# Another order of stages for the experts of a mixture layer, on one core

## The chip, the cores and the metric

The kernel runs on one core of one Trainium2 chip. The metric is the device time of one execution, in microseconds (us). Before the change it is 1570.87 us, the median of 3 runs (1569.34 to 1571.96). All rows below come from one profiled execution, which took 1567.68 us; its span, from the first to the last instruction, is 1565.9 us.

## The reference

One encoder layer on 512 tokens of width 1024, in float32: two groups of attention heads, cross-attention into 256 memory tokens, and a mixture of 32 experts. Only the last part is touched. Each token goes to its 4 best experts:

```python
logits = x @ w_router + b_router
top_logits, top_idx = lax.top_k(logits, 4)
gates = softmax(top_logits)
# for each expert e, over the tokens that chose it:
gu = xb @ w_gate_up[e] + b_gate_up[e]          # 1024 -> 2048
gate, up = split(gu); gate = min(gate, 7); up = clip(up, -7, 7)
y = ((up + 1) * gate * sigmoid(1.702 * gate)) @ w_down[e] + b_down[e]   # 1024 -> 1024
out[token] += gate_of(token, e) * y
```

An expert has 12 MiB of weights, and each of the 32 is read whole from the device's main memory.

## The kernel before

The layer's front part ends near 478 us. From there the 32 experts follow one another, one expert a stage. Experts are ranked by how many tokens chose them. A string, `PLAN` (line 34), names the kind of each stage, and `_rank` (line 36) deals the ranks out: the biggest experts to the stages of kind D, then E, W, M, N and Q, within a kind in the order of their stages. A kind says how many slots for tokens the stage has (`KINDS`, line 33): D 256, E 128+32, W 128, M 64+32, N 64, Q 32. Stage 0 is a W for one fixed expert.

Narrow stages (M, N, Q; class `NarrowStage`) multiply in plain float32 straight from the weights as they land, with 64 or 32 slots side by side in the array. A wide stage (W, E, D; `WideStage`, `DoubleStage`) first splits every row of weights into a high and a low part, `eh` on ScalarE (ACT, line 342) and `el` on VectorE (DVE, line 343), and does three products for each (lines 1424 to 1426).

A stage's weights are 12 chunks of 1 MiB (`wchunk`): eight of `w_gu` (gate and up), four of `w_dn` (down). SyncE (SP) issues their loads in order (line 1355), into 12 buffers in rotation, so that a load waits until the chunk 12 places before it has been used: in a narrow stage by the last product that reads it, in a wide stage by the split. While stage s runs, the loads of stage s+1 are issued, and the first ones of s+2. Behind a W or E, the last two chunks of a narrow stage go into other buffers (`load_late`, line 1658).

On TensorE (PE) the order is written by hand (`run_stage`, line 1670). A stage is: eight or more pieces of the up product, the activation (`act`: lines 1397 to 1400 on ACT and DVE), the transposes of its result `h` (`turn`), and the down product. The tokens' rows for the next stage are transposed three pieces before the end of the up product (`prep`). To cover the activation, the next stage's first pieces are done ahead: some before `turn`, some before the down product. This needs room in the six accumulators of 2 KiB per partition (PSUM banks):

```python
AHEAD = {"Q": (3, 1), "N": (2, 1), "M": (2, 2), "W": (1, 1), "E": (1, 1), "D": (1, 0)}   # 42
BANKS = {"Q": 1, "N": 2, "M": 3, "W": 4, "E": 5, "D": 4}                                  # 44
    if s in (0, len(PLAN) - 1, len(PLAN)) or BANKS[PLAN[s - 1]] + BANKS[PLAN[s]] > 6:     # 53
        return 0, 0
```

So a W gets two pieces ahead behind an N or a Q, and none behind an M or a W. The other engines' orders are set by a scheduler. With the plan before, the stages without pieces ahead are 11 (W behind M), 21 (W behind M), 22 (W behind W) and the last. In every fourth stage (s % 4 == 1) the tables of slots for four later stages are made beside the up product.

Of the kernel before, what the change touches and what calls it, by code (L numbers as in the profile page):

```python
# [30 lines left out]


KINDS = {"D": (2, 0, 0), "E": (1, 0, 1), "W": (1, 0, 0), "M": (0, 1, 1), "N": (0, 1, 0), "Q": (0, 0, 1)}
PLAN = "WNQDQNQEQMMWQMNMQNMQMWWNWNWNNMQQ"
_left = list(range(31))
_rank = {k: iter([_left.pop(0) for _ in range(PLAN.count(k) - (k == "W"))]) for k in "DEWMNQ"}
STAGES = [(k, 31 if i == 0 else next(_rank[k])) for i, k in enumerate(PLAN)]

# [11 lines left out]
def ahead(s):  # L50


    if s in (0, len(PLAN) - 1, len(PLAN)) or BANKS[PLAN[s - 1]] + BANKS[PLAN[s]] > 6:
        return 0, 0
    return AHEAD[PLAN[s]]


def ahead_chunks(s):

    n = sum(ahead(s))  # L60
    return 1 + max(k for _, k in PIECES[2 if PLAN[s] == "M" else 1][:n]) if n else 0


CAP = {k: 128 * v[0] + 64 * v[1] + 32 * v[2] for k, v in KINDS.items()}
assert PLAN[-1] == "Q" and sorted(r for _, r in STAGES) == list(range(32))

# [1812 lines left out]
```

## Time and profile before

| | |
|---|---|
| median of 3 runs | 1570.87 us |
| profiled execution, its span | 1567.68 us, 1565.9 us |
| PE busy | 1414.9 us (90%) |
| DVE, ACT, POOL busy | 48%, 35%, 11% |
| moved by DMA | 474.76 MB, mean 303 GB/s |
| loads of `wchunk` | 256 + 128 of 1 MiB |

How to read it: busy time is counted for each engine, and "idle before" is the time in which an engine stood still before an instruction, with the one that released it. Matmuls are pipelined, so a busy PE may still be slowed. From the slice at 470 us on, the load of the weights runs beside the stages. A stage is taken here to end where ACT begins its last copy of the result, `ys<-gu` (lines 140, 294 and 1496); with that the stages from 7 on are:

| stage | kind | from, us | stage | kind | from, us |
|---|---|---|---|---|---|
| 7 | E | 718.3 | 20 | M | 1137.4 |
| 8 | Q | 772.9 | 21 | W | 1177.5 |
| 9 | M | 788.4 | 22 | W | 1222.8 |
| 10 | M | 825.2 | 23 | N | 1265.5 |
| 11 | W | 859.9 | 24 | W | 1298.0 |
| 12 | Q | 902.0 | 25 | N | 1334.4 |
| 13 | M | 918.3 | 26 | W | 1367.5 |
| 14 | N | 954.4 | 27, 28 | N, N | 1403.9 |
| 15 to 19 | M Q N M Q | 978.8 | 29 to 31 | M Q Q | 1453.3 |

### The profile page before, as it was taken

The numbers are of one execution on the slowest core, as the hardware profiler recorded it, in microseconds if no ns is written. First come the engines' busy times: TensorE is split into PE (matmuls) and PEld (weight loads), VectorE is DVE, ScalarE is ACT, GpSimd is POOL, SyncE is SP. The second block draws the span as 40 slices with busy tenths as digits, with TensorE's granted clock in tenths as the row PEclk, the third lists the DMA queues.
The fourth block names the chain that finished last, engine by engine and source line by source line (L and its number), as shares of the span: only waits on it lengthen the run. The fifth ranks groups of instructions, "written<-read, shape, count | busy, mean of one in ns | idle before, by whom it ended". The sixth has DMA issues, their size and how long they took to land. (4 is left out here: it accounts for less than half of the span.)

```text
span 1565.9 us, 24737 instructions
## 1 busy us (share of the span) xinstructions
PE 1414.9 (90%) x9775; PEld 934.7 (60%) x9775; DVE 754.8 (48%) x1207; ACT 554.9 (35%) x799; POOL 175.2 (11%) x153
## 2 busy tenths in 40 slices
PE   8999999899998989978999999878888989899962
PEld 6898899788996557625644743323336756463321
DVE  6667797865478536225422720110118846462005
ACT  6667584444225333214301611000115645351001
POOL 1000000310031010020011011111002000111014
PEclk9999999999999999999999999999989999999975
DMA  6121245242449998799999999999999899999994
GB/s 214 43 66 58 73 133 192 68 150 80 189 173 375 392 396 323 270 404 418 405 416 388 409 406 412 416 412 416 412 411 389 335 408 357 398 362 354 416 412 179
DMA packets 111766, 474.76 MB, mean 303 GB/s; under 512 B 12577, under 2 KB 47801, under 8 KB 64032
## 3 DMA queue, kind: packets, MB, share of 16 engines
q1 hardware_dynamic: 98464, 446.66, 71.8%
q0 software_dynamic: 10848, 21.99, 5.3%
q10 hardware_dynamic: 2336, 4.50, 0.8%
q8 instruction: 78, 1.28, 0.3%
q14 instruction: 40, 0.33, 0.1%
HBM read 460.87 MB, written 17.32 MB: 305 GB/s over the span
## 5 line engine op out<-in xcount | busy, mean ns | idle before, releaser
L343 DVE TENSOR_TENSOR el<-wchunk,eh 128x1024 fp32r<-128x1024 f32 x192 | 232.5, 1224 | 99.0 <-ACT eh L342 97.0
L342 ACT ACTIVATE eh<-wchunk 128x1024 fp32r<-128x1024 f32 x192 | 200.4, 1059 | 108.4 <-PE gu L1426 101.3
L115 PE MATMUL gu<-wchunk,x64t 128*64 128x512 f32 x960 | 222.6, 602 | 4.6 <-DMA wchunk<-w_gu 4.5
L115 PE MATMUL gu<-wchunk,x32t 128*32 128x256 f32 x2176 | 137.9, 393 | 23.4 <-DMA wchunk<-w_gu 23.4
L1398 DVE TENSOR_SCALAR h<-gu 128x512 f32<-128x512 f32 (+1 forms) x50 | 29.7, 599 | 251.1 <-PE gu L115 146.0
L1409 POOL DMA_INDIRECT acc<-ys,idx x41 | 67.6, 1648 | 698.1 <-ACT ys L140 362.7
L115 PEld LDWEIGHTS gu<-wchunk,x64t 128*64 128x64 f32 x960 | 63.8, 137 | 123.2 <-issue 111.8
L1424 PE MATMUL gu<-eh,xg 128*128 128x512 f32 x288 | 117.3, 411 | 10.5 <-ACT eh L342 6.4
L115 PE MATMUL gu<-wchunk,h64t 128*64 128x512 f32 x480 | 113.3, 615 | 14.4 <-DMA wchunk<-w_dn 14.4
L1425 PE MATMUL gu<-el,xg 128*128 128x512 f32 x288 | 117.8, 409 | 4.0 <-DVE el L343 3.5
L1426 PE MATMUL gu<-eh,xg 128*128 128x512 f32 x288 | 117.0, 406 | 4.8 <-DVE xg L343 4.8
L115 PEld LDWEIGHTS gu<-wchunk,x32t 128*32 128x32 f32 x2176 | 64.8, 112 | 87.3 <-DMA wchunk<-w_gu 37.4
L140 ACT ACTIVATE ys<-gu,gate 128x256 f32<-128x256 f32 (+1 forms) x32 | 18.3, 573 | 219.9 <-PE gu L115 219.9
L343 DVE TENSOR_TENSOR wl<-w,wh 128x1024 fp32r<-128x1024 f32 (+2 forms) x67 | 80.8, 1220 | 31.7 <-ACT wh L342 31.3
L342 ACT ACTIVATE wh<-w 128x1024 fp32r<-128x1024 f32 (+2 forms) x67 | 67.0, 1017 | 53.7 <-PE qmps L416 15.0
L115 PE MATMUL gu<-wchunk,h32t 128*32 128x256 f32 x1088 | 71.4, 410 | 14.9 <-DMA wchunk<-w_dn 14.0
L115 PEld LDWEIGHTS gu<-wchunk,h64t 128*64 128x64 f32 x480 | 33.0, 140 | 85.8 <-issue 61.0
L1397 ACT ACTIVATE sg<-gu 128x512 f32<-128x512 f32 (+1 forms) x50 | 26.2, 524 | 137.8 <-PE gu L115 73.8
L1424 PEld LDWEIGHTS gu<-eh,xg 128*128 128x128 f32 x288 | 55.7, 194 | 27.4 <-ACT eh L342 8.6
L1404 DVE TENSOR_SCALAR brow<-masks,perm 128x128 fp32r<-128x128 f32 x49 | 12.8, 284 | 118.3 <-PE gu L106 116.7
L1425 PEld LDWEIGHTS gu<-el,xg 128*128 128x128 f32 x288 | 55.6, 193 | 21.0 <-DVE el L343 8.6
L1426 PEld LDWEIGHTS gu<-eh,xg 128*128 128x128 f32 x288 | 55.8, 194 | 17.9 <-DVE xg L343 5.4
(430 smaller groups left out, 2761.5 us busy)
## 6 DMA issues: line engine op xcount, KB each, us to landing
wchunk<-w_gu SPq DMA_DIRECT2D x256, 1024.0 KB, 18.1
wchunk<-w_dn SPq DMA_DIRECT2D x128, 1024.0 KB, 18.8
w<-w_in SPq DMA_DIRECT2D x22, 512.0 KB, 4.6
w<-w_kv SPq DMA_DIRECT2D x16, 512.0 KB, 3.4
w<-w_out SPq DMA_DIRECT2D x8, 512.0 KB, 3.5
w<-w_q SPq DMA_DIRECT2D x8, 512.0 KB, 4.1
w<-w_o SPq DMA_DIRECT2D x8, 512.0 KB, 4.2
relb<-relT SPq DMA_DIRECT2D x8, 256.0 KB, 2.8
```

Of the source, the lines that this page charges most:

```text
L115: self.k.nc.tensor.matmul(ps[r], xt[:, k % c, k // c, :], row[:, q * self.w:(q + 1) * self.w], start=False, stop=last, skip_group_check=True)
L140: self.k.nc.scalar.activation(ys, self.y, AF.Copy, scale=tab[1])
L342: nc.scalar.activation(hi, src, AF.Copy)
L343: nc.vector.tensor_tensor(lo, src, raw(hi), op=ALU.subtract)
L1397: nc.scalar.activation(s, gp, AF.Sigmoid, scale=1.702)
L1398: nc.vector.tensor_scalar(h, up, -6.0, 8.0, op0=ALU.max, op1=ALU.min)
L1404: self.nc.vector.tensor_scalar(b, mask, col, None, op0=ALU.mult)
L1409: self.nc.gpsimd.indirect_dma_start(out=self.acc.rearrange("t (h d) -> (t h) d", h=n), out_offset=bass.IndirectOffsetOnAxis(ap=idx, axis=0 ...
L1424: nc.tensor.matmul(out, ah[:, k, :], bh, start=False, stop=False, skip_group_check=True)
L1425: nc.tensor.matmul(out, ah[:, k, :], bl, start=False, stop=False, skip_group_check=True)
L1426: nc.tensor.matmul(out, al[:, k, :], bh, start=False, stop=last, skip_group_check=True)
```

## The change

```diff
-PLAN = "WNQDQNQEQMMWQMNMQNMQMWWNWNWNNMQQ"
+PLAN = "WNQDQNQEQMMNWQMNWQMMNWQMNWNWNMQQ"
```

The counts of the kinds are the same (6 W, 1 D, 1 E, 7 M, 8 N, 9 Q), so every rank keeps a kind with the same slots. Stages 0 to 10 keep their kinds. From there the W stages stand at 12, 16, 21, 25 and 27 (before: 11, 21, 22, 24, 26), each behind an N; the stages without pieces ahead are now 0 and 31 alone. Nothing else in the file is changed; how many pieces are ahead, which chunks are loaded late and where the tables are made follow from the string.

On PE, the entry into the first wide stage behind stage 10. Before, stage 10 (M) runs into stage 11 (W): `x64t`, `x32t` are the M's tokens, `h_...` its activations, `xgt` the transposes of the W's tokens, line 1480 opens the W's four accumulators.

```order
L1441 MATMUL xgt<-ident,xg_4670 128x128 x8
L115 MATMUL gu<-wchunk,x64t 64x512 x8
L1441 MATMUL h_7829<-ident,h 128x128 x4
L1441 MATMUL h_7836<-ident,h 128x128 x2
L106 MATMUL gu<-bt,brow 128x512
L115 MATMUL gu<-wchunk,h64t 64x512 x16
L106 MATMUL gu<-bt,brow 128x256 x2
L115 MATMUL gu<-wchunk,h32t 32x256 x32
L1480 MATMUL gu<-bt,brow 128x512 x4
L1424 MATMUL gu<-eh,xg 128x512
```

Now stage 11 (N) runs into stage 12 (W):

```order
L1441 MATMUL xgt<-ident,xg_4670 128x128 x8
L115 MATMUL gu<-wchunk,x64t 64x512 x8
L1480 MATMUL gu<-bt,brow 128x512 x4
L1424 MATMUL gu<-eh,xg 128x512
L1425 MATMUL gu<-el,xg 128x512
L1426 MATMUL gu<-eh,xg 128x512
```

The accumulators of the W are opened before the transposes of the stage ahead of it: twelve wide products stand between the N's up product and the transposes of its `h`, and twelve more behind those, where nothing stood between.

On DVE, the place where the W's tokens are split (`xg<-xgt`), in a narrow stage ahead of a wide one. Before, at stage 23 (N, behind the W of stage 22; `el` are the splits of the next W's weights):

```order
L1497 TENSOR_SCALAR ys<-gu,gate 128x512
L1398 TENSOR_SCALAR h<-gu 128x512
L1399 SCALAR_TENSOR_TENSOR h<-gu,h 128x512
L1400 SCALAR_TENSOR_TENSOR h<-sg,h 128x512
L343 TENSOR_TENSOR el<-wchunk,eh 128x1024 x3
L343 TENSOR_TENSOR xg<-xgt,xg 128x512 x2
L343 TENSOR_TENSOR el<-wchunk,eh 128x1024
```

Now, at stage 20 (N, behind the M of stage 19), and alike at stages 11, 15 and 24; at stage 26 (N behind a W) it stands as before:

```order
L1404 TENSOR_SCALAR brow<-masks,perm 128x128 x3
L343 TENSOR_TENSOR xg<-xgt,xg 128x512 x2
L1398 TENSOR_SCALAR h<-gu 128x512
L1399 SCALAR_TENSOR_TENSOR h<-gu,h 128x512
L1400 SCALAR_TENSOR_TENSOR h<-sg,h 128x512
L343 TENSOR_TENSOR el<-wchunk,eh 128x1024 x4
```

The split of the tokens stands ahead of the N's activation and of the W's first weights, where it stood behind three of their splits.

## Rows read from the trace of the kernel before

**Rows 1.** The page, part 2: GB/s in 40 slices of the span.

```profile
GB/s 214 43 66 58 73 133 192 68 150 80 189 173 375 392 396 323 270 404 418 405 416 388 409 406 412 416 412 416 412 411 389 335 408 357 398 362 354 416 412 179
```

**Rows 2.** Windows: stretch, length, five engines' busy us, PEclk, DMA share, GB/s.

```profile
978.80:1137.40 158.60, 131.30 (x1149) 51.44 (x1145) 18.16 (x46) 13.83 (x29) 16.87 (x12) 0.98 1.02 414
825.20:902.00 76.80, 72.13 (x483) 44.12 (x476) 39.97 (x45) 32.05 (x38) 6.99 (x4) 0.98 1.00 398
1177.50:1403.90 226.40, 210.87 (x934) 140.75 (x935) 150.49 (x175) 115.99 (x128) 20.57 (x14) 0.96 0.96 375
```

**Rows 3.** Loads issued from 978.8 to 1137.4: xcount, KB, median us to landing.

```profile
wchunk<-w_gu SPq DMA_DIRECT2D x38, 1024.0 KB, 20.9
wchunk<-w_dn SPq DMA_DIRECT2D x22, 1024.0 KB, 21.0
```

**Rows 4.** Loads issued from 1298.0 to 1334.4 (stage 24).

```profile
wchunk<-w_gu SPq DMA_DIRECT2D x10, 1024.0 KB, 6.3
wchunk<-w_dn SPq DMA_DIRECT2D x4, 1024.0 KB, 8.5
```

**Rows 5.** Waits of SP in stage 24: total us, times, longest.

```profile
SPq L1355 <- DVE el L343: 19.5, 7, 6.2
SPq L1355 <- PE gu L115: 6.4, 3, 3.4
```

**Rows 6.** Waits of PE from 978.8 to 1137.4.

```profile
PE gu L115 <- DMA wchunk<-w_dn: 14.1, 17, 1.4
PE gu L115 <- DMA wchunk<-w_gu: 12.2, 18, 1.5
```

**Rows 7.** Windows: single stages, 7 to 11 and 13.

```profile
718.30:772.90 54.60, 49.97 (x400) 35.01 (x404) 31.98 (x36) 25.19 (x29) 4.60 (x3) 0.94 1.01 417
772.90:788.40 15.50, 15.50 (x200) 8.17 (x196) 1.75 (x5) 2.14 (x6) 1.57 (x1) 1.00 1.03 386
788.40:825.20 36.80, 36.80 (x339) 15.85 (x335) 9.10 (x25) 3.86 (x8) 7.29 (x6) 1.00 1.02 416
825.20:859.90 34.70, 31.15 (x258) 12.90 (x251) 8.69 (x14) 7.08 (x12) 3.94 (x2) 0.95 0.97 384
859.90:902.00 42.10, 40.98 (x226) 31.22 (x227) 31.28 (x32) 24.98 (x27) 3.05 (x2) 1.00 1.02 409
918.30:954.40 36.10, 36.10 (x301) 14.40 (x295) 8.38 (x23) 3.61 (x8) 5.33 (x4) 1.00 1.02 417
```

**Rows 8.** Windows: stages 20 to 26.

```profile
1137.40:1177.50 40.10, 34.21 (x258) 13.70 (x259) 8.70 (x14) 7.17 (x12) 5.02 (x3) 0.87 0.98 402
1177.50:1222.80 45.30, 39.79 (x182) 31.19 (x183) 35.96 (x47) 27.95 (x31) 5.88 (x3) 0.92 0.93 370
1222.80:1265.50 42.70, 42.62 (x188) 31.14 (x187) 34.14 (x34) 26.30 (x29) 3.00 (x2) 1.00 0.96 376
1265.50:1298.00 32.50, 28.09 (x118) 13.66 (x117) 12.35 (x14) 9.70 (x12) 2.62 (x2) 0.89 1.01 397
1298.00:1334.40 36.40, 36.19 (x158) 25.67 (x159) 26.25 (x27) 21.17 (x23) 1.60 (x1) 1.00 0.94 360
1334.40:1367.50 33.10, 27.99 (x137) 13.42 (x136) 15.54 (x26) 9.70 (x12) 4.68 (x4) 0.95 1.00 394
1367.50:1403.90 36.40, 36.19 (x158) 25.67 (x159) 26.25 (x27) 21.17 (x23) 2.79 (x2) 1.00 0.94 357
```

**Rows 9.** Waits of PE in stage 20.

```profile
PE h L1441 <- DVE h L1400: 3.2, 2, 2.4
PE gu L115 <- DMA wchunk<-w_gu: 2.8, 2, 1.4
```

**Rows 10.** PE in order of time: start, us, instruction, [idle before and releaser].

```profile
1206.08 1.10 PE L1441 MATMUL ht<-ident,h 128*128 128x128 f32 x4 [3.23 <-DVE h L1400]
1209.28 1.10 PE L1441 MATMUL ht<-ident,h 128*128 128x128 f32 x4 [2.10 <-DVE h L1400]
...
1279.27 0.50 PE L1424 MATMUL gu<-eh,xg 128*128 128x512 f32 x1 [2.04 <-ACT xg L342]
...
1282.43 0.79 PE L1426 MATMUL gu<-eh,xg 128*128 128x512 f32 x1 [2.38 <-DVE xg L343]
```

**Rows 11.** Waits of PE in stage 7 (E).

```profile
PE gu L1424 <- ACT eh L342: 2.6, 1, 2.6
PE gu L1425 <- DVE el L343: 1.9, 2, 1.1
```

## The prediction

> **What bounds the kernel now.** I read the page's slices first: from the twelfth slice on (about 470 us) the core moves close to 400 GB/s, and the late dips to 335, 357, 362 and 354 lie where the W stages stand close together [rows 1]. Then the windows. From 978.8 to 1137.4, stages of kinds M, Q and N, the core moves 414 GB/s and PE is busy for 131.3 of 158.6 us; from 1177.5 to 1403.9, where four of six stages are W, PE is busy for 210.9 of 226.4 us and the core moves 375 GB/s [rows 2]. So two limits take turns. In the first stretch the load of weights is the limit: PE waits 26.3 us for `wchunk` [rows 6], and a load lands 21 us after it was issued, behind others [rows 3]. In the second PE is: a load lands 6.3 us after its issue [rows 4], nothing is ahead of it, and SP waits for a split or a product to free a buffer, 25.9 of 36.4 us in one W stage [rows 5]. Time in which the loads stand still because all 12 buffers are full is lost for good, since every stage, whatever its kind, needs the same 12 MiB.
>
> How long a stage's load takes: 60 loads were issued in 158.6 us [rows 2, 3], 2.64 us each, so 31.7 us for 12. How far the loads can run ahead of PE: what a load waits in the queue is 20.9 us with the buffers empty and 6.3 us with them full [rows 3, 4], so 14.6 us is the store that the buffers hold.
>
> **The account of before.** I go from stage to stage and add what PE needs beyond 31.7 us (the store fills), or below (it empties, and at zero PE waits). What goes beyond 14.6 us is lost to the loads. An E needs 54.6 us, so the store is full behind stage 7; a Q needs 15.5 and empties it [rows 7]. Then M 36.8 (+5.1), M 34.7 (+3.0), W 42.1 (+10.4): 18.5, of which 3.9 are lost [rows 7]. The next Q empties it, and up to 1137.4 the loads are the limit. Stage 20 needs 40.1 less 2.8 of waiting for weights, 37.3 (+5.6) [rows 8, 9]; W 45.3 (+13.6) loses 4.6; W 42.7 loses 11.0; N 32.5 loses 0.8; W 36.4 loses 4.7; N 33.1 loses 1.4; W 36.4 loses 4.7 [rows 8]. Together 31.1 us. The trace's own figure: at 414 GB/s the bytes of the stretch 825.2 to 902.0 would take 76.8 x 398/414, 3.0 us less than it took, and those of 1177.5 to 1403.9 would take 21.3 us less [rows 2]: 24.3. The account is too hard by 0.78, and I scale by that.
>
> **The change, part by part.** (1) The W stages move apart. What a stage computes and loads is unchanged, so nothing is added to PE's products or to the bytes. (2) The entries into wide stages. Removed are the three without pieces ahead: the waits for the activation at stage 20 (3.2 us [rows 9]) and at the turn of stage 21 (3.2 and 2.1 us [rows 10]), and one like the first at stage 10, whose busy time is 3.5 us short of its length [rows 7]; 12 us. What they hid comes to light: a W behind an N waited for the split of its tokens, 2.0 on ACT and 2.4 on DVE [rows 10], and there are now five of these and not two. At four of them the split stands ahead of the N's activation and of the weights' splits, so most of the wait should go; then the first weights' split is late next, as in E (2.6 for `eh`, 1.9 for `el` [rows 11]). I take 3 us at four entries and 4.4 at the fifth: 16.4 against 8.8 + 12. PE gains about 4 us, and only where it is the limit. So an N ahead of a W needs 32.8 (mean of the two [rows 8]) less 1.4, 31.4. (3) SP: the first chunk of a W is now loaded ahead of the four `w_dn` chunks of the N before it; the number of loads is the same. One more narrow stage, 28, is behind a W and takes its last two chunks late, into buffers that the W's tokens leave free after the up product; that adds to the store, and I cost it at nothing. (4) The tables of slots fall in the same stage numbers, of which 13 and 17 are now Q: their few DVE instructions lie beside the wait for weights there.
>
> The unknown is what a W needs when its chunks come just in time, as they will behind a DMA-limited stretch. Below: 36.4, as at stages 24 and 26 [rows 8]. Above: the one wide stage that stood in such a stretch, E, lost 4.5 us to `eh` and `el` [rows 11]; with 0.5 for the row that waits behind them, 41.4. Behind stage 8 neither is nearer, so I take the middle, 38.9.
>
> **The account of after**, with M ahead of N or M 36.1 (as stage 13 [rows 7]): stages 9 to 12: 5.1, 9.5, 9.2, 16.4, lost 1.8. Q empties. M, N, W: 4.4, 4.1, 11.3, nothing lost. Q empties. M, M, N, W: 4.4, 8.8, 8.5, 15.7, lost 1.1. Q empties. M, N, W, N (33.1), W: 4.4, 4.1, 11.3, 12.7, 19.9, lost 5.3. The last N, M, Q, Q find the store full and are limited by the loads again. Lost 8.2 in place of 31.1; 22.9 x 0.78 = 17.9 us gained. With W at 36.4 only 0.3 is lost, a gain of 24.0; with 41.4 the losses are 18.2, a gain of 10.1. The profiled execution took 1567.7, so 1549.8 by its own time; the median stands 3.2 above it: **1553 us**. By itself this case reaches from 1547 to 1561.
>
> **A rule that speaks against it.** In the stretch limited by the loads the core moved 414 GB/s [rows 2]. The Trainium skill, SBUF — State Buffer (Summary: rules for kernel authors), says that transfers between device memory and SBUF are to be estimated with about 358 GB/s. By it, an estimate, a stage's 12.58 MB would take 35.1 us, the 357 to 376 GB/s of the W stages would be the memory's own limit, and no order of stages would gain; the trace disagrees by its 414, for 158.6 us on end.
>
> **The rivals.** (A) The W stages themselves slow the loads: the splits of ACT and DVE read and write the same memory that the DMA engines fill, and the W stages show the 357 to 376. Then the losses only move with them, and the time stays at 1571. For it: the dips follow the W's. Against: stage 11, a W with as much DVE and ACT work, ran at 409, and E at 417 [rows 7], and in W stages SP is seen waiting for buffers [rows 5]. The Trainium skill's rule above would give this result too.
> (B) Slower: the chain chunk, `eh`, `el`, product is the limit of each W that starts with empty buffers. The loss grows with every us: the account of after reaches the 31.1 of before when a W needs 44.2 us. At 47 the losses are 45.4, and the time is 0.78 x 14.3 = 11 us longer, 1582. For it: stage 21, the W with tables beside it, needed 45.3, and stages 21 and 25 are such W's now. Against: 5.3 of those 45.3 were the waits at its turn [rows 10], which pieces ahead now cover, and the chunks of a W come 2.64 us apart while its products need 36.2/12 = 3.0 for each [rows 8], so the store fills during the stage.
> (C) Half of the clock: at entries and in Q stages where PE waits, the granted clock fell (0.87 to 0.92 in stages 20, 21 and 23 [rows 8], between the levels of 2.4 and 1.2 GHz). With more waits for weights it falls more often; where the loads are the limit that is covered. If each of five W's begins slow, at 2 us each, W needs about 41: 1561, in the forecast's range.
> (D) The loads never stand still, and the bytes bring the whole of 24.3 and the 4 us of PE: 1543.
>
> **How the numbers follow.** The forecast with its range (C within it) 0.72, D 0.08, A 0.10, B 0.06, and 0.04 for a small gain of 4 to 9 us (W near 43). A measurement of this kernel can tell about 0.2%, 3 us, from no change. Faster: 0.72 + 0.08 + 0.04 + 0.01 of A, 0.85. Same: 0.09. Slower: 0.06. The range of 1543 to 1567 leaves out A, B and the outer half of D, about 2 in 10.
>
> **What would show it.** Right: windows over stages 11 to 27 at 405 GB/s or more, with no W stage below 390; PE waiting for `wchunk` in the Q's behind a W (13, 17, 22); a load's time to landing above 8 us in the W's but the last; waits for `xg` at four entries below 3 us. Wrong: W stages near 360 GB/s while loads land 15 us and more after issue (A); W stages of 43 us and more with PE waiting for `eh` and `el` (B); a gain with the GB/s unchanged, which would put it in the tail behind stage 28, where I expect the same work.

## The result, and the profile after

The changed kernel takes 1554.74 us (median of 4 runs, 1550.96 to 1556.08) against 1571.18 us (4 runs, 1569.34 to 1571.96) for the kernel before: the ratio is 0.9895, 95% interval 0.9877 to 0.9912. That is 16.4 us less; the forecast was 17.9 less. The profiled execution took 1556.08 us, its span is 1554.5 us. Of all executions reported below one is left out: 2031.44 us, at a granted clock of 0.647, of the kernel without late chunks.

Where the time was saved. Cut at the last copy of `ys` as before, stages 9 to 30 lasted from 788.4 to 1507.9 us before, 719.5 us, and last from 791.0 to 1495.2 now, 704.2 us: 15.3 us less, in two profiled spans that are 11.4 us apart (the medians are 16.4 apart). Ahead of stage 9, where the order is the same, after's execution took 2.6 us longer; behind stage 30 it took 58.0 us to the end of the span and takes 59.3. The two windows, of before:

```profile
788.40:1507.90 719.50, 657.01 (x4490) 334.94 (x4482) 256.36 (x374) 191.94 (x250) 81.51 (x61) 0.97 1.00 396
```

and of after (length, the five engines' busy us, PEclk, DMA share, GB/s):

```profile
791.00:1495.20 704.20, 654.93 (x4490) 337.50 (x4482) 255.57 (x374) 190.46 (x250) 79.93 (x61) 0.97 1.02 407
```

PE has the same 4490 products and the same busy time within 2.1 us. What differs is the rate of the loads, 396 GB/s and now 407; by length x rate it is the same 285 to 287 MB. PE's waits for weights in the same two windows, of before:

```profile
PE gu L115 <- DMA wchunk<-w_dn: 18.9, 22, 1.9
PE gu L115 <- DMA wchunk<-w_gu: 16.8, 21, 1.7
```

and of after:

```profile
PE gu L115 <- DMA wchunk<-w_gu: 7.5, 6, 3.0
PE gu L115 <- DMA wchunk<-w_dn: 6.7, 7, 2.1
```

These fell from 35.7 to 14.2 us. All its other waits together (for activations, for splits of tokens and weights, for the tables' `oh`) did not fall: 26.0 us before, 34.4 now.

The slices of the page show the higher rate too. Of the late dips of [rows 1], 335, 357 and 362 lay at W stages and are gone. The fourth, 354, lay at 1409 to 1448 us, in stages 27 and 28, both N: it is the hole of stage 28 (last section), which is left, now 361 in the 37th slice together with the end of stage 27:

```profile
GB/s 202 42 82 46 83 124 204 55 165 82 163 163 365 367 394 318 257 407 412 421 401 411 412 418 405 411 417 406 398 409 418 406 418 412 411 405 361 397 412 141
```

The windows of after that answer to [rows 2] and [rows 8]: first stages 11 to 26 in one, then N and W in pairs (stages 11 and 12, 15 and 16, 20 and 21, 24 and 25), then 26 and 27 (N and W):

```profile
862.70:1382.10 519.40, 477.12 (x3128) 253.00 (x3128) 202.63 (x282) 153.71 (x196) 55.12 (x39) 0.96 1.02 411
862.70:890.90 28.20, 26.10 (x113) 12.60 (x113) 8.29 (x10) 6.65 (x9) 1.56 (x1) 0.94 1.02 409
890.90:929.40 38.50, 34.88 (x198) 26.13 (x199) 29.74 (x30) 23.80 (x27) 1.55 (x1) 1.00 1.01 416
990.20:1017.00 26.80, 24.89 (x113) 11.43 (x113) 8.28 (x10) 6.92 (x10) 1.56 (x1) 1.00 1.02 408
1017.00:1056.70 39.70, 36.16 (x198) 27.07 (x199) 29.74 (x30) 23.75 (x26) 2.96 (x2) 0.96 1.02 417
1155.90:1184.10 28.20, 26.04 (x113) 12.51 (x111) 8.28 (x10) 6.64 (x10) 1.56 (x1) 0.94 1.02 409
1184.10:1225.60 41.50, 37.17 (x215) 27.27 (x216) 32.38 (x42) 23.81 (x27) 7.05 (x3) 0.96 1.02 415
1280.10:1306.70 26.60, 24.77 (x113) 11.35 (x111) 8.29 (x10) 6.84 (x9) 2.61 (x2) 1.00 1.02 410
1306.70:1350.50 43.80, 39.18 (x178) 26.95 (x179) 32.41 (x42) 23.87 (x26) 5.79 (x5) 0.96 1.02 416
1350.50:1382.10 31.60, 27.62 (x117) 13.20 (x116) 12.35 (x14) 9.71 (x12) 1.62 (x1) 0.89 1.01 408
1382.10:1418.80 36.70, 36.22 (x158) 25.70 (x159) 27.31 (x28) 21.18 (x23) 1.57 (x1) 1.00 0.99 392
```

Four W stages now run at 415 to 417 GB/s, where those of before, close together, had 357 to 376 [rows 8]. They last as long as then in part (43.8 us in stage 25), with PE idle in them for 3.5 to 4.6 us. They need more time than their 31.7 us of loads; the loads go on beside them because the buffers have room. Only the last, 27, is at 392; it is 36.7 us long with PE busy for 36.2 of them, as the W's in stages 24 and 26 before.

On SP, stage 25 of after answers to [rows 5]:

```profile
SPq L1355 <- DMA wchunk<-w_gu: 22.5, 13, 2.1
SPq L1355 <- DMA wchunk<-w_dn: 7.0, 4, 2.0
SPq L1355 <- PE gu L115: 1.3, 2, 0.9
SPq L1355 <- DVE el L343: 0.6, 1, 0.6
```

Before, SP stood for 25.9 us in a W because a split or a product had not freed a buffer; here it is 1.9 us, and 29.5 us are waits for earlier loads to land. Not every W is like this one. In stages 12 and 16 the waits for a buffer are below 3 us as well, but in stage 21 they are 16.6 us (still at 415 GB/s) and in stage 27 26.8. Over stages 11 to 26 together, the two largest of these waits before:

```profile
SPq L1355 <- DVE el L343: 137.3, 51, 9.8
SPq L1355 <- PE gu L115: 73.3, 43, 9.5
```

and after:

```profile
SPq L1355 <- PE gu L115: 23.2, 19, 4.7
SPq L1355 <- DVE el L343: 12.0, 9, 3.0
```

With the smaller ones, SP stood 220.5 us for buffers before and 39.4 now. On PE, from 862.7 to 1382.1 (in place of [rows 6, 9 to 11]):

```profile
PE gu L1425 <- DVE el L343: 16.7, 16, 2.1
PE gu L1424 <- ACT eh L342: 7.1, 5, 1.7
PE gu L115 <- DMA wchunk<-w_gu: 5.8, 5, 3.0
PE gu L115 <- DMA wchunk<-w_dn: 4.2, 4, 2.1
PE slot L1301 <- DVE oh L1294: 4.1, 7, 1.5
PE gu L1424 <- ACT xg L342: 2.0, 1, 2.0
PE gu L1426 <- DVE xg L343: 1.9, 1, 1.9
```

The waits for the tokens' split (`xg`) are left at one entry, that of stage 27; waits for the weights' splits (`el`, `eh`), 23.8 us in sum, have come up in the W's. In this stretch waits of PE change places without changing the time, as the experiments show.

### The profile page after: what moved, and what is told of

The parts are those of the page before. It is cut to its first block, busy times and chain, and to the rows that moved or that the text cites. A ratio compares the mean times of both kernels' runs of the same rounds, so it can differ in the third digit from the quotient of the medians.

```text
span 1554.5 us, 24729 instructions
## 1 busy us (share of the span) xinstructions
PE 1419.1 (91%) x9775; PEld 942.2 (61%) x9775; DVE 753.2 (48%) x1207; ACT 553.5 (36%) x799; POOL 174.5 (11%) x153
## 5 line engine op out<-in xcount | busy, mean ns | idle before, releaser
L1425 PE MATMUL gu<-el,xg 128*128 128x512 f32 x288 | 122.8, 426 | 15.7 <-DVE el L343 15.3
L1424 PE MATMUL gu<-eh,xg 128*128 128x512 f32 x288 | 121.1, 425 | 13.7 <-ACT eh L342 11.6
L1426 PE MATMUL gu<-eh,xg 128*128 128x512 f32 x288 | 119.7, 416 | 1.9 <-DVE xg L343 1.9
L115 PE MATMUL gu<-wchunk,h64t 128*64 128x512 f32 x480 | 107.9, 597 | 5.3 <-DMA wchunk<-w_dn 5.2
L343 DVE TENSOR_TENSOR wl<-w,wh 128x1024 fp32r<-128x1024 f32 (+2 forms) x67 | 80.8, 1221 | 31.7 <-ACT wh L342 31.4
L115 PE MATMUL gu<-wchunk,h32t 128*32 128x256 f32 x1088 | 69.7, 405 | 9.6 <-DMA wchunk<-w_dn 9.0
L1424 PEld LDWEIGHTS gu<-eh,xg 128*128 128x128 f32 x288 | 57.3, 200 | 34.0 <-ACT eh L342 18.0
L1397 ACT ACTIVATE sg<-gu 128x512 f32<-128x512 f32 (+1 forms) x50 | 26.3, 525 | 132.9 <-PE gu L115 69.3
L1426 PEld LDWEIGHTS gu<-eh,xg 128*128 128x128 f32 x288 | 58.0, 202 | 15.5 <-DVE xg L343 2.6
L1425 PE MATMUL gu<-el,ht 128*128 128x512 f32 x144 | 57.6, 400 | 5.9 <-DVE el L343 5.9
```

What stands on the lines that cost most here:

```text
L115: self.k.nc.tensor.matmul(ps[r], xt[:, k % c, k // c, :], row[:, q * self.w:(q + 1) * self.w], start=False, stop=last, skip_group_check=True)
L343: nc.vector.tensor_tensor(lo, src, raw(hi), op=ALU.subtract)
L1397: nc.scalar.activation(s, gp, AF.Sigmoid, scale=1.702)
L1424: nc.tensor.matmul(out, ah[:, k, :], bh, start=False, stop=False, skip_group_check=True)
L1425: nc.tensor.matmul(out, ah[:, k, :], bl, start=False, stop=False, skip_group_check=True)
L1426: nc.tensor.matmul(out, al[:, k, :], bh, start=False, stop=last, skip_group_check=True)
```

## The experiments

Two theories. **S (store):** the gain comes from the loads, which stand still less, because no group of stages needs more PE time than the 12 buffers can lend. **P (PE's waits):** it comes from the waits at the entries into W stages, which pieces ahead and an earlier token split take away. Each kernel was timed against the kernel before on its chip; a difference in us below is from the ratio and 1571.

**The W's apart, but without pieces ahead.** The order of the change, with each of its four first W's behind an M, where no pieces fit ahead:

```diff
-PLAN = "WNQDQNQEQMMNWQMNWQMMNWQMNWNWNMQQ"   # the change
+PLAN = "WNQDQNQEQMMWNQMWNQMMWNQMWNNWNMQQ"
```

> The changed plan with the first four pairs N W turned round into W N (from stage 9 on: MMWNQMWNQMMWNQMWNNWNMQQ). The wide stages stand as far apart as in the change, but four of them come behind an M, with no piece ahead (before: three such entries; the change: none). Theory S (the loads: the gain comes from a store of loaded weights that no longer overflows): account with M 34.7, W 42.1, N 24.4 as before: 3.9 us lost at each of two W's, 7.8 x 0.78 = 6 us in place of 24, so about 18 us faster than before, 1551 to 1558, and W stages above 400 GB/s. Theory P (the entries: the gain is TensorE's waits at entries without pieces ahead): four such entries in place of three, 4 us slower than before, 1573 to 1577.

Measured: 1552.75 us (1550.33 to 1554.03), ratio 0.9887 (0.9866 to 0.9908), the whole gain. PE waits from 858.9 to 1416.2:

```profile
PE h L1441 <- DVE h L1400: 10.1, 6, 2.4
PE gu L1425 <- DVE el L343: 9.4, 8, 2.1
```

and the window of that stretch, with one of its W's:

```profile
858.90:1416.20 557.30, 520.01 (x3307) 278.46 (x3308) 227.92 (x306) 173.06 (x216) 56.59 (x40) 0.96 1.01 408
987.50:1031.60 44.10, 42.74 (x186) 30.93 (x187) 31.43 (x32) 25.21 (x27) 3.33 (x2) 1.00 1.02 412
```

The wait for the activation is back, 10.1 us, and each of the four W's takes 44 us; nothing of it reaches the time, since the core loads at 412 beside it. P is refuted here.

**Pieces ahead at every entry, but the W's together.** All five W's behind an N with pieces ahead, one N between each two:

```diff
+PLAN = "WNQDQNQEQMMMNWNWNWNWNWNQMQMQMQMQ"
```

> A plan with all five W's close together, each behind an N and so with pieces ahead (from stage 9 on: MMMNWNWNWNWNWNQMQMQMQMQ); no entry without pieces ahead, as in the change. Theory S: the store fills in the three M's and overflows in each pair from then on: 28 us lost in the account, x 0.78 = 22, nearly the 24 of before: 1566 to 1572, with 360 to 380 GB/s in the W stages. Theory P: as the change or better, 1551 to 1556.

Measured: 1573.33 us (12 runs, 1570.91 to 1576.20), ratio 1.0024 (1.0011 to 1.0037): slightly slower than before, although no entry is without pieces ahead. The other thing that the change gives, the early split of the tokens, four of these entries lack, since their N stands behind a W. PE waits from 925.3 to 1242.5:

```profile
PE gu L1426 <- DVE xg L343: 9.0, 4, 2.4
PE gu L1424 <- ACT xg L342: 8.1, 4, 2.0
```

So its time alone doesn't decide between S and P. Windows of the whole group of W's, then of its third, fourth and fifth:

```profile
925.30:1242.50 317.20, 293.11 (x1307) 182.91 (x1307) 193.59 (x234) 147.30 (x167) 32.32 (x20) 0.95 0.99 391
...
1068.10:1104.70 36.60, 36.32 (x175) 25.82 (x176) 28.84 (x39) 21.15 (x24) 7.91 (x4) 1.00 0.98 373
1136.50:1172.40 35.90, 35.61 (x158) 25.64 (x159) 26.25 (x27) 21.16 (x23) 1.59 (x1) 1.00 0.96 370
1204.50:1242.50 38.00, 36.54 (x183) 25.95 (x183) 30.34 (x43) 21.14 (x24) 6.35 (x4) 1.00 0.92 353
```

PE is busy throughout the later W's and the rate falls from one to the next, as the store would have it. The first two went at 415 and 390 GB/s. By its bytes the group loses 317.2 x (1 - 391/414) = 17.6 us. Its end (an M ahead of the last Q) costs it more: by itself such an end was 8 us slower, as an experiment below shows. Without these 8 us it would be some 4 us faster than before, near the 6 by which its bytes lose less than the 23.7 of before.

**The change without pieces ahead in W's.**

```diff
-    ... BANKS[PLAN[s - 1]] + BANKS[PLAN[s]] > 6:
+    ... BANKS[PLAN[s - 1]] + BANKS[PLAN[s]] > 6 or PLAN[s] == "W":
```

> The changed plan, with no piece ahead at the five entries into wide stages (a condition in ahead()). Theory S: TensorE waits 3 to 5 us more at each entry, but the loads are the limit and the account stays under 14.6 us but for the last W: within 5 us of the change, 1553 to 1560. Theory P: five entries without pieces ahead against three before: 8 us slower than before, 1575 to 1582.

Measured: 1553.46 us (1550.81 to 1555.91), ratio 0.9891 (0.9869 to 0.9912): no difference to the change. The stretch of stages 11 to 26 and its first W (the five W's took 44.0 to 48.3 us, at 415 to 418 GB/s, the last at 385):

```profile
862.20:1375.70 513.50, 472.11 (x3100) 245.09 (x3099) 197.40 (x277) 149.72 (x192) 59.77 (x39) 0.96 1.02 411
884.60:928.60 44.00, 41.44 (x226) 31.03 (x226) 34.64 (x34) 27.98 (x30) 1.55 (x1) 1.00 1.02 418
```

PE waits 9.6 us for activations here, and 11.6 for the weights' splits where the change has 23.8: the pieces ahead exchange one wait for another. So the pieces ahead, which the change brings to every W, are worth nothing in this order. All of PE's waits for activations and splits over stages 11 to 26 are 18.6 us before, 27.7 in the change and 26.1 here, and 21.2 over stages 11 to 27 with the W's behind M's: none of the three kernels that gain has less of them than before. S is right here and P is not.

**A W moved alone.** From the plan before, one of the two W's that stood next to each other goes to stage 15:

```diff
-PLAN = "WNQDQNQEQMMWQMNMQNMQMWWNWNWNNMQQ"   # before
+PLAN = "WNQDQNQEQMMWQMNWMQNMQMWNWNWNNMQQ"
```

> The plan of before with one W moved: the second of the pair W W goes to the place behind the N of stage 14 (from stage 9 on: MMWQMNWMQNMQMWNWNWNNMQQ). Theory S: the account loses 18.0 in place of 31.1 us, x 0.78 = 10 us faster than before: 1557 to 1564. Theory P: one of three entries without pieces ahead goes, a third of the gain of 16: 1563 to 1567.

Measured: 1558.82 us (1555.01 to 1562.51), ratio 0.9924 (0.9903 to 0.9945), 12 us of the change's 16. The moved W runs at 415 GB/s and the one in stage 22 at 414 (376 before, [rows 8]); those in 24 and 26 keep 370 and 359. P saw at least 1563.

**Two products for three in the wide stages**, in the order before and in that of the change. The third product (line 1426, the high weights times the low part of the tokens) is left out, so a W needs less of PE while its loads and splits stay:

```diff
-        nc.tensor.matmul(out, ah[:, k, :], bl, start=False, stop=False, skip_group_check=True)
-        nc.tensor.matmul(out, al[:, k, :], bh, start=False, stop=last, skip_group_check=True)
+        nc.tensor.matmul(out, ah[:, k, :], bl, start=False, stop=last, skip_group_check=True)
```

> The plan of before, with the third product of each row in the wide stages left out (L1426), so that the result lacks that part. A W then needs about 33 us (24 us of products, its 24 splits on VectorE 29 us) in place of 36 to 42, close to the 31.7 of its loads; it is compared with the next kernel, the changed plan with the same left out. Theory S: with W's that fit their loads the order of stages no longer matters: the two kernels differ by 0 to 6 us. Theory P: the three entries keep their cost: they differ by 12 to 16 us. Either way both are far under 1555, about 1510 to 1530, since stages 0, 3 and 7 shrink too.

> The changed plan with the same third product left out, to be compared with the kernel before it. Theory S: 0 to 6 us faster than that one. Theory P: 12 to 16 us faster.

Measured: 1537.54 us (1536.96 to 1537.67), ratio 0.9789 (0.9766 to 0.9812), with the order before; 1534.19 us (1531.17 to 1536.48), ratio 0.9769 (0.9744 to 0.9794), with the change's. Their difference is 3.3 us, where P wanted 12 to 16: with PE faster in the W's, the two orders are nearly the same. The absolute times were missed, both are above 1510 to 1530. One W of the order before (stage 24), to be held against 36.4 us at 360 GB/s [rows 8]:

```profile
1268.70:1301.60 32.90, 30.37 (x122) 17.41 (x124) 25.28 (x28) 21.29 (x24) 1.60 (x1) 1.00 1.01 415
```

DVE and ACT split for as long (25.3 and 21.3 us, before 26.3 and 21.2) in less time, and the loads go at 415. So the splits do not slow the loads; PE did, by keeping the buffers: on the page of before ACT's splits (line 342) stood 101.3 us for products of line 1426, and a buffer is free only when it is split.

**No late chunks.** The last chunks of a narrow stage behind a W go into the 12 buffers like the others (`late` gives an empty list):

```diff
-        return self.order(s)[10:] if wide else []
+        return []
```

> The changed plan without late loads: behind a wide stage the last two chunks of a narrow stage go into the 12 rotating buffers too. Theory S: the store behind a W is 2 chunks, 5.3 us, smaller; the account of the change reaches the brim at stages 12, 21 and 27, so up to 3 x 5.3 x 0.78 = 12 us are lost, and nothing where a Q behind the W waits for weights anyway: 1556 to 1566. Theory P: the order on TensorE is the same: 1553 to 1556.

Measured: 1553.08 us (4 runs, 1552.03 to 1554.56), ratio 0.9886 (0.9863 to 0.9910). S had expected a loss and was wrong: stages 11 to 26 stay at 411 GB/s. Either these two chunks are not 5.3 us of store, or the 12 buffers hold more than the 14.6 us of the account; no run tells which.

**A Q between the last W's.** The last N W N W of the change leaves 27 at 392 GB/s; a Q between them should have brought that back:

```diff
+PLAN = "WNQDQNQEQMMNWQMNWQMMNWQMNWQNWNMQ"
```

> A plan that sets one of the three last narrow stages between the last two pairs (from stage 9 on: MMNWQMNWQMMNWQMNWQNWNMQ). Theory S: the one overflow that the trace of the change still shows (393 GB/s in stage 27, 2 us of loads) goes; 1551 to 1556. Theory P: the same entries and the same time as the change, but for 2 us at the one entry behind a W where the tokens' split came late: 1552 to 1556. The two are not told apart by this; it is to see whether the plan can be bettered.

Measured: 1562.88 us (1559.83 to 1565.45), ratio 0.9959 (0.9939 to 0.9979): a miss, 7 us above the upper end of what was expected and 10 slower than the change by the ratios (8 by the medians). Its last expert product ends at 1522.9 us, earlier than the 1531 of the change, yet its span ends later. What is late is the sum: stage 30, now an M, adds its results to `acc` in two transfers one behind the other, and the final norm reads `sums` behind them. On POOL:

```profile
1501.61 1.59 POOL L1409 DMA_INDIRECT acc<-ys,idx  x1 [13.82 <-ACT ys L140]
1512.65 1.57 POOL L1409 DMA_INDIRECT acc<-ys,idx  x1 [9.44 <-DMA acc<-ys,idx]
1521.00 1.09 POOL L1752 DMA_INDIRECT own<-acc,idx  x1 [6.78 <-issue]
1522.09 1.59 POOL L1737 DMA_DIRECT2D sums<-acc  x2
```

**The M ahead of the last Q, by itself.** The change with only its stages 29 and 30 exchanged, to tell this from the W of 28 (T: the tail's additions; W: the wide stage):

```diff
-...NWNWNMQQ
+...NWNWNQMQ
```

> The changed plan with stages 29 and 30 in the other order, Q M Q in place of M Q Q at the end. The kernel with a Q between the last pairs also ended in M Q, and was 8 us slower than the change, though its last product was over earlier; its final sums were read later, behind the M's second addition. Theory T (the end is set by the last but one stage's additions, then the reading of the sums and the norm): 1560 to 1565. Theory W (that kernel lost in its W of stage 28, 365 GB/s, which had the leftover tables beside it): as the change, 1553 to 1556.

Measured: 1562.52 us (1561.75 to 1564.66), ratio 0.9946 (0.9930 to 0.9962); T is right. Its row on DVE:

```profile
1526.32 1.88 DVE L670 BATCH_NORM_STATS2 bnst<-sums 128x6 f32<-128x512 f32 x3 [13.05 <-DMA sums<-acc]
```

and the change's:

```profile
1518.72 0.42 DVE L1398 TENSOR_SCALAR h<-gu 128x256 f32<-128x256 f32 x1 [31.94 <-ACT sg L1397]
...
1519.98 1.87 DVE L670 BATCH_NORM_STATS2 bnst<-sums 128x6 f32<-128x512 f32 x3
```

With the M in stage 30 the norm waits 13.05 us for `sums`; in the change it follows the last activation without a wait. It begins 6.3 us later, and by as much the profiled execution is longer (1562.39 against 1556.08).

**The leftover tables elsewhere.** Stage 28 builds the last tables, and the loads have a hole there (below). Building them in stage 4, or in stage 3, was to close it:

```diff
-        if s == n - 4:
+        if s == 4:      # and in the other kernel: if s == 3:
```

> The changed plan, with the leftover tables made in stage 4 and not in stage 28. In both traces the core moves only 130 to 170 GB/s for 6 to 7 us in stage 28, when these tables are written out and read back by small transfers. Theory: in stage 4 the loads stand still anyway (276 GB/s, buffers full), so the hole costs nothing there, and 3 to 6 us are gained on the change: 1548 to 1552. Rival: the last stages hide it, since the sums set the end: as the change, 1553 to 1556.

> The changed plan with the leftover tables made in stage 3, the D. With them in stage 4 the hole in the loads left stage 28 (404 GB/s, and 5.3 us were gained from there to stage 30) but came back in stage 5 (340 GB/s, 6.5 us lost), because it fell when the loads were the limit again. In stage 3 the buffers are full and the loads stand still later in the same stage (200 GB/s from 606 us on), so a hole ahead of that costs nothing. Theory: 4 to 6 us faster than the change measured on the same chip: ratio to it near 0.997, about 1549. Rival (the hole or the work of the tables costs as much in D): as the change.

The change itself ran again beside the second one:

> The change as it is, measured beside the kernel with the tables in stage 3. 1551 to 1557.

Measured: in stage 4 1557.97 us (1554.00 to 1561.01), ratio 0.9910 (0.9892 to 0.9928); in stage 3 1555.73 (1554.79 to 1557.94), ratio 0.9904 (0.9880 to 0.9927); the change 1553.74 (1552.11 to 1555.49), ratio 0.9889 (0.9865 to 0.9912). No gain in either. The hole left stage 28, and stages 28 to 30 were 5.2 and 7.2 us shorter (the second beside the change measured with it), but stage 5 grew from 29.3 us at 402 GB/s to 34.6 at 340 in the first, and stage 3 from 75.5 to 80.1 us in the second. In the second the additions take up the rest (POOL):

```profile
1476.11 1.60 POOL L1409 DMA_INDIRECT acc<-ys,idx  x1 [13.33 <-ACT ys L140]
1487.48 1.56 POOL L1409 DMA_INDIRECT acc<-ys,idx  x1 [9.78 <-DMA acc<-ys,idx]
1496.06 1.55 POOL L1409 DMA_INDIRECT acc<-ys,idx  x1 [7.02 <-DMA acc<-ys,idx]
```

The last stands at 1496.06, where the change has it too (1495.99; 1494.85 in the change measured again), although the stages ended earlier: here each of the last two waits for the one before it to land, where in the change the last was released by ACT's `ys`.

## Why the prediction was right

**The account (the store).** Right, in kind and nearly in size. Moving W's apart gains whether their entries are covered or not (0.9887 with the W's behind M's, 0.9891 without pieces ahead, 0.9924 for one W alone). The kernel with the W's together (1.0024) had late splits of tokens and a slower end as well; there it is the rate, falling to 353 GB/s, that speaks for the store. Forecast were 8.2 us of loss in the account, 6.4 by the scale of 0.78. By the bytes, stages 11 to 26 lose 519.4 x (1 - 411/414) = 3.8 us and stage 27 36.7 x (1 - 392/414) = 2.0: 5.8. The same reckoning for the stretch of 11 to 26 before, 544.0 us at 396 GB/s, gives 23.7 (forecast 24.3). The difference, 17.9, is what the forecast had; that it agrees to a tenth is luck, since rates rounded to 1 GB/s leave each of these sums open by 0.7 us. With the measured lengths of all stages, less their waits for weights, the account overflows at stages 21 (2.0 us) and 27 (2.4) alone, and these are the two W's in which SP stood for buffers for more than 3 us. Of the 17.9, 15.3 are found in stages 9 to 30, into which, by length x rate, 1.7 MB more of loads fall now, some 4 us, give or take 2. The profiled executions themselves are only 11.6 us apart: after's stands at the top of its runs, with stage 9 beginning 2.6 us later behind the same order, and before's below its median.

One premise of the account is not shown. The store of 14.6 us came from a landing time of 20.9 us "with the buffers empty". In that stretch SP waited 114.0 us for earlier loads to land and 2.8 for buffers, and 20.9 us are eight loads of 2.64: the time shows how many loads were on their way, and not how much 12 buffers hold. No run measures the store, and the kernel without late chunks leaves its size open. Two readings were off without effect on the sum: the twelfth slice ends, and does not begin, near 470 us, and the dip of 354 is not at a W.

**What a W needs, 38.9 us.** They took 38.5, 39.7, 41.5, 43.8 and 36.7 with their waits; the N's ahead of them took 28.2, 26.8, 28.2, 26.6 and 31.6 where 31.4 was forecast. The 31.4 came from two N's that stood behind a W [rows 8]; the fifth N stands there too and has it, and the four behind an M are 3 to 5 us shorter by this cut. I had not seen that a stage's length depends on the kind ahead of it. The pairs are 66.7, 66.5, 69.7, 70.4 and 68.3 us against 70.3 (72.0 for the fifth), so the sum that the account needs was right to 4 us, mostly on the safe side. Stages 21 and 25, 41.5 and 43.8, lie above the 41.4 that was the upper bound for a W; the shorter N's made up for it, which was not foreseen. The two W's with tables beside them, 21 and 25, are the longest, as at stage 21 before [rows 8].

**Step (2), the entries.** What it said of `xg` came about: at four entries the wait is gone, at the fifth it is 2.0 and 1.9 us. That PE gains about 4 us did not. The weights' splits are late next, for more than the 3 us allowed at each of four entries. The entry into stage 21 on PE:

```profile
1185.76 0.50 PE L1424 MATMUL gu<-eh,xg 128*128 128x512 f32 x1 [1.73 <-ACT eh L342]
...
1187.02 0.80 PE L1425 MATMUL gu<-el,xg 128*128 128x512 f32 x1 [0.77 <-DVE el L343]
```

Over the stretch they sum to 23.8 us (the rows above), where 12 were allowed. The term was mis-sized and did not enter the time, since over this stretch the loads are the limit: the kernel without pieces ahead, with 9.6 us of waiting for the activation and half of the waits for splits, took 1553.46.

**Step (3), the late chunks.** "Adds to the store, and I cost it at nothing": nothing is what it is, also where it is taken out altogether (1553.08). My reason was too kind to it.

**Step (4), the tables.** In stages 13 and 17 PE waited 2.5 and 1.6 us for `oh`, beside no wait for weights in 13 and 3.7 us in 17. It was exposed, not hidden as I had said; what it cost is not shown by itself. I named the Q's 13, 17 and 22 as places where PE waits for `wchunk`; only 17 showed it. The others of these waits are in the M's behind (3.0 us in 14, 1.1 in 18, 2.2 in 23).

**The sign of the landing times** (above 8 us in the W's but the last) can't be read in the change: its trace has none for these loads. In the same order without pieces ahead they are 19.8 to 21.0 us in the first four W's, with the W's behind M's 12.6 to 16.9; in the fifth W of the former, 12.5 and 14.1.

**The rule that spoke against it.** Four W's, stages of 39 to 44 us with all their splits, moved 415 to 417 GB/s. The Trainium skill's figure of about 358 GB/s for such transfers (SBUF — State Buffer, Summary: rules for kernel authors) does not hold for this kernel, one core at work: no run here has it as a limit.

**The rivals.** A (the W's slow the loads) is refuted by these, and by the two-product kernel at 415 with the same splits. B (the chain of chunk, `eh`, `el`, product) had its threshold at 44.2 us for a W. It didn't come to that with the change, and with W's of 44 us (behind M's) and of 44 to 48 (without pieces ahead) nothing was lost either. The threshold was reckoned with an N of 31.4 us beside each W; what counts is the pair, and the N's are shorter. C (half of the clock): the granted clock was 0.96 to 1.00 in the W's and 0.89 to 1.00 in the N's ahead of them, so parts were at the level of 1.2 GHz; whatever it cost lies within a stretch whose pace the loads set. D (everything) missed: the 5.8 us above are still lost, and the 4 us of PE did not come.

## What to carry to other kernels

Where loads run through a ring of buffers beside stages of unlike compute, add up from stage to stage what each stage's compute needs beyond its load time, cap the sum at what the ring holds and floor it at zero: what is cut off at the cap is lost, and the order of stages is chosen to keep it small, with the waits of the compute engine inside load-limited stages counted at nothing. Time to landing (21 us where the loads were the limit, 6 where buffers were full, here) tells which limit a stage has, and so does what the issuing engine waits for: earlier loads or buffers. How deep the ring is it does not tell. Before shortening the last stages, look for the chain that runs beside them: here a stage with two dependent additions next to the last cost 8 us.

## What the runs showed of the hardware that was not expected

Additions to one tensor in main memory, each waiting for the one before, start 8.6 to 11.4 us apart at the end of these kernels (1476.11, 1487.48, 1496.06 above). The kernel that differs from the change by such a stage next to the last alone was 8 us slower.

In stage 28 the loads fall below half of their rate for some 6 us, in both orders. Before:

```profile
1439.00:1446.00 7.00, 7.00 (x58) 3.17 (x56) 1.66 (x3) 0.60 (x1) 0.00 (x0) 1.00 1.08 170
```

and after:

```profile
1433.00:1439.00 6.00, 6.00 (x53) 2.60 (x51) 0.29 (x1) 0.60 (x1) 0.00 (x0) 1.00 1.11 130
```

The DMA engines show as fully busy (share 1.08 and 1.11) while they move 170 and 130 GB/s. It follows two small transfers of the leftover tables (17 KB and 0.5 KB, issued by POOL at 1425.90 and 1426.51 in after), and it left stage 28 when these were built in stage 4. So it goes with the tables. Before, the hole ends within 2 us of the landing of the second of the two (issued at 1435.18, 11.3 us to landing), and so does the one of the kernel with the tables in stage 4 (issued at 665.16, 15.4 us to landing; back to 381 GB/s from 682). That points at this transfer; whether it is the cause, and why, was not tried.
